# Hymba layer on one core: the second token tile's mixed rows loaded earlier, a clamp joined with the product behind it, one stage's side loads begun later

## The chip, the cores and the metric

The kernel runs on one core of one Trainium2 chip. The metric is the device time of one execution in microseconds (us), the median of several runs. TensorE (PE) multiplies matrices; its weight loads (PEld) overlap with the multiplications. VectorE (DVE), ScalarE (ACT) and GpSimd (POOL) work elementwise, and SyncE (SP) issues the DMAs, each in the order in which they stand in its queue.

## The reference: what is computed

One layer for 1024 tokens of width 1024, float32. A convolution group (256 channels) and an attention group (12 query heads, 4 key heads, head size 64, three gated branches: compressed blocks, selected blocks, sliding window) read the same normalised input. Their outputs are concatenated into the mixed rows, go through one output projection and are added to x; a dense SwiGLU block and a last norm follow.

```python
h = rms_norm(x, attn_norm)
z = h @ w_in
a_conv, q, kc_r, vc_r, ks, vs, kw, vw, g = jnp.split(z, splits, axis=-1)
conv_out = conv_mixer(a_conv, conv_w, conv_b, conv_ln_g, conv_ln_b)
kc = compress(kc_r, cmp_k_pe, cmp_k_w1, cmp_k_w2)
vc = compress(vc_r, cmp_v_pe, cmp_v_w1, cmp_v_w2)
gates = jax.nn.sigmoid(g)
nsa_out = nsa_attention(q, kc, vc, ks, vs, kw, vw, gates)
mix = jnp.concatenate([conv_out, nsa_out], axis=-1)
x = x + mix @ w_out
h = rms_norm(x, ffn_norm)
gate, up = jnp.split(h @ w_gate_up, 2, axis=-1)
return x + (silu(gate) * up) @ w_down
```

## The kernel before

Tokens are cut into eight tiles of 128; tiles 0 to 3 form the first half, 4 to 7 the second. Matrix products are made at higher precision by splitting: an operand is cast to a high part (`w_hi`, `ph`, `ah`; ACT) and the remainder is subtracted (`w_lo`, `pl`, `al`; POOL for weights, DVE for activations), and three matmuls high·high, high·low, low·high replace one. `load_w` (L219 to L237) does this for a weight block: DMA into `w_raw` (L229), cast (L230), subtraction in pieces (L234). Values that cross a stage are written to DRAM and read back: queries `q_d`, keys `ks_d` and `kw_d`, values `vs_d` and `vw_d`, compressed probabilities `pc_d`, and the mixed rows `mix_d[w, channel, token]`, where w is 0 for the high part and 1 for the low one.

The first part of the kernel projects the first half of the tokens (`project_d`, `values`), makes the compressed keys and values (`compress`, `compress_v`) and runs the convolution's end (`conv_tail`, which stores its 256 channels of the mixed rows, L665) with compressed-block scoring (`cmp_stage`, one call for a key group g and a pair of token tiles qt, sixteen in all) beside it. Such side work is given to `drive.side(generator, at)`: `drive.run` steps through the main work, counts its modelled time `drive.t`, and takes a step of a side generator when its due time has come. `cmp_stage` loads queries (L678), makes scores (L686), their minimum over 64 blocks (L693), clamps the six minima to at most CLAMP (L694, tile `cm`), multiplies by the heads' slopes (L696, tile `bm`) and uses the product as bias of the six exponentials on ACT (L700); POOL scales them (L704, L708), PE transposes (L714) and the result goes to `pc_d`.

Then attention over the first half runs, woven with `fill_b`, which yields the projections of the second half and at its end the convolution's input part (`conv_in`). Attention takes one tile and one branch after the other: scores `s` (L851, L855), a reduction with ALiBi on DVE (L859), exponentials on ACT (L866), their sum and reciprocal on DVE (L870, L871), scaling by sum and gate on POOL (L876), transposes `pt` (L882), a split into `ph` and `pl` (L240), the product with the values (L910, L911) beside the compressed branch (L905), and the sum of the branches (`ou`, L914, L915; `oh`, L920, L921), which is stored to `mix_d` (L929). Keys are loaded for each group and branch at L789.

The output projection of the first half (`out_proj`, L1226 `wo`) takes for each token tile twelve matmuls: four blocks of 128 channels, three products. Its rows come from `mix_in` (L1203), which loads tiles 1 to 3 of the high and low part into buffers of the tag `act`, tile 1 first and then tiles 2 and 3 in one piece, and for tile 0 from `first_mix` (L1212), which is called at step 60 of `conv_in` and uses two buffers (`cacc`) of the convolution's pool `py`. The buffers of `act` are the ones in which the normalised input lies until the last matmul of `conv_in`.

Nothing in the code fixes the final order of instructions: a scheduler that simulates a timeline of all engines and queues orders each engine's instructions by its own model. The rows of the order quoted below are its result.

Of the kernel before, what the change touches and what calls it, by code (L numbers as in the profile page):

```python
# [12 lines left out]
F32 = mybir.dt.float32  # L13
# [75 lines left out]
def tile_hymba(ctx: ExitStack, tc, x, attn_norm, w_in, conv_w, conv_b, conv_ln_g, conv_ln_b,  # L89
# [582 lines left out]
    def cmp_stage(g, qt):  # L672
        i0 = qt * 2
        if qt < 2 and g < 3:
            qc = p2.tile([P, REP, 256], F32R, tag="xt", name="qc", bufs=2)
        else:
            qc = t3([P, REP, 256], F32R, "qc", 1)
        sp.dma_start(qc.bitcast(F32), q_d[g * 192:(g + 1) * 192, :, i0 * P:(i0 + 2) * P]  # L678
                     .rearrange("(r d) w t -> (d w) r t", d=HD))
        s = t3([P, 6, 64], F32, "cs", 2)  # L680
        s4 = s.rearrange("p (i r) n -> p i r n", r=REP)
        yield 0.0
        for il in range(2):
            sb = bank("sc", "s")
            for r in range(REP):
                pe.matmul(sb[:, r * P:(r + 1) * P], qc[:, r, il * P:(il + 1) * P], kc[:, g], start=True, stop=True)  # L686
            sb4 = sb[:, :384].rearrange("p (r c n) -> p r c n", r=REP, c=2)
            dve.tensor_tensor(s4[:, il], sb4[:, :, 0, :], cb[:, i0 + il, :].unsqueeze(1).to_broadcast([P, REP, 64]),
                              op=ALU.add)
            dve.tensor_tensor(s4[:, il], s4[:, il], sb4[:, :, 1, :], op=ALU.add)  # L690
        yield 0.7
        m = p1.tile([P, 6], F32, tag="cm", name="cm", bufs=3)
        dve.tensor_reduce(m, s, axis=AX.X, op=ALU.min)  # L693
        dve.tensor_scalar(m, m, CLAMP, None, op0=ALU.min)  # L694
        bm = p1.tile([P, 6], F32, tag="bm", name="bm", bufs=3)
        dve.tensor_tensor(bm.rearrange("p (i r) -> p i r", r=REP), m.rearrange("p (i r) -> p i r", r=REP),  # L696
                          slo[:, g * REP:(g + 1) * REP].unsqueeze(1).to_broadcast([P, 2, REP]), op=ALU.mult)
        l = p1.tile([P, 6], F32, tag="cl", name="cl", bufs=3)
        for u in range(6):
            act.activation(s[:, u, :], s[:, u, :], AF.Exp, scale=-SLOPES[g * REP + u % REP], bias=bm[:, u:u + 1],  # L700
                           accum_out=l[:, u:u + 1])
        dve.tensor_scalar(l, l, 1e-30, None, op0=ALU.max)
        dve.reciprocal(l, l)
        pool.tensor_tensor(s, s, l.unsqueeze(2).to_broadcast([P, 6, 64]), op=ALU.mult)  # L704

        pg = t3([P, 6, 64], F32, "pg", 2)
        gt = gates[:, i0:i0 + 2, g * 9:(g + 1) * 9].rearrange("p i (r b) -> p i r b", b=3)[:, :, :, 0]
        pool.tensor_tensor(pg.rearrange("p (i r) n -> p i r n", r=REP), s4,  # L708
                           gt.unsqueeze(3).to_broadcast([P, 2, REP, 64]), op=ALU.mult)
        yield None  # L710
        pct = t3([P, 3, 2, P], F32R, "pct", 2)
        pt = bank("pt", "t")
        for v in range(3):
            pe.transpose(pt[:, v * P:(v + 1) * P], pg[:, 2 * v:2 * v + 2, :], ident)  # L714
        yield 0.33
        pt3 = pt[:, :384].rearrange("p (v q) -> p v q", q=P)
        for e in range(2):
            src = pt3[e * 64:(e + 1) * 64]
            act.copy(pct[0:64, :, e, :], src)
            dve.tensor_sub(pct[64:128, :, e, :], src, pct[0:64, :, e, :].bitcast(F32))  # L720
        sp.dma_start(pc_d[g, qt], pct.bitcast(F32).rearrange("p v e q -> p (v e q)"))
        done.add(("pc", g, qt))

        if qt < 2:
            return
        im = p1.tile([P, 2, 64], F32, tag="im", name="im", bufs=2)
        pool.tensor_tensor(im, s4[:, :, 0, :], s4[:, :, 1, :], op=ALU.add)
        pool.tensor_tensor(im, im, s4[:, :, 2, :], op=ALU.add)
        ib = p1.tile([P, 2, 16], F32, tag="ib", name="ib", bufs=2)
        im4 = im.rearrange("p i (j n) -> p i j n", n=4)  # L730
        dve.tensor_reduce(ib, im4, axis=AX.X, op=ALU.add)
        dve.tensor_tensor(ib[:, :, 1:16], ib[:, :, 1:16], im4[:, :, 0:15, 3], op=ALU.add)
        dve.tensor_tensor(ib, ib, ft[:, i0:i0 + 2, :], op=ALU.add)
        if qt == 2:
            chosen[g] = p1.tile([P, 4, 16], F32, tag="us", name="us", bufs=2)
        us = chosen[g][:, i0 - 4:i0 - 2, :]
        for il in range(2):
            mx = p1.tile([P, 8], F32, tag="mx", name="mx", bufs=2)
            dve.max(mx, ib[:, il, :])
            dve.match_replace(us[:, il, :], mx, ib[:, il, :], 4.0 * NEG)  # L740
        dve.tensor_tensor(us, us, ib, op=ALU.is_equal)
        if qt == 3:
            yield None
            ut = bank("ut", "t")
            pe.transpose(ut[0:64, :P], chosen[g], ident)
            bt = p1.tile([64, P], F32, tag="im", name="bt", bufs=2)
            yield 0.11
            dve.tensor_scalar(bt, ut[0:64, :P], BIG, None, op0=ALU.mult)
            sp.dma_start(bias_d[g].rearrange("v j q -> (v j) q"), bt)
            done.add(("bias", g))  # L750
# [242 lines left out]
    def stages_in(g):  # L993
        for qt in range(2):
            gaps = iter(STAGE_GAPS)
            for _ in cmp_stage(g, qt):
                yield next(gaps)
# [23 lines left out]
    def mixed_in(a, b):  # L1021
# [31 lines left out]
    turn[1] = "t"  # L1053
    drive.run(in_turn(compress(*xv, first, cmp_v_w2, "z", kv),
                      [project_d(first, dst, r, (0,)) for dst, r in ((ks_d, 0), (kw_d, P))], 24))
    drive.side(stages_in(3))
    drive.run(project_d(first, ks_d, P, (0,)))
    compress_v(*kv)
    p2_stack.close()
# [5 lines left out]
    def fill_b():  # L1065
        f1 = Feed([q_load(0), q_load(1)] + value_loads(C_VS, 0) + [q_load(2)] + value_loads(C_VW, 18)
                  + [q_load(m) for m in (3, 4, 5)] + kv_loads() + conv_loads())
        for m in (0, 1):
            yield from project_d(f1, q_d, m * P, (1,), True)
        yield from values(f1, 0, vs_d, 1)  # L1070
        done.add(("q", 0))
        yield from project_d(f1, q_d, 2 * P, (1,), True)
        done.add(("q", 1))
        yield from values(f1, 18, vw_d, 1)
        done.update({("v", 0), ("v", 1)})
        for m in (3, 4):
            yield from project_d(f1, q_d, m * P, (1,), True)
        done.add(("q", 2))
        yield from project_d(f1, q_d, 5 * P, (1,), True)
        done.add(("q", 3))  # L1080
        for dst in (kw_d, ks_d):
            yield from project_d(f1, dst, 0, (1,))
        done.add(("kv", 0))
        for dst in (kw_d, ks_d):
            yield from project_d(f1, dst, P, (1,))
        done.add(("kv", 1))
        for n, d in enumerate(conv_in(f1, 1)):
            if n == 60:
                first_mix()
            yield d  # L1090
        done.add(("conv", "in"))

# [102 lines left out]
    def mix_in(si, kq, p, tag="act", tokens=True):  # L1195
        assert mixed(si, kq)
        t0, n = SETS[si][0] * P, len(SETS[si]) * P
        mix = [p.tile([P, 4, n], F32R, tag=tag, name="mix", bufs=2) for _ in range(2)]
        src = [mix_d[w, kq * 512:(kq + 1) * 512, t0:t0 + n].rearrange("(k p) t -> p k t", p=P) for w in range(2)]
        for a, b in ((1, 2), (2, 4)) if tokens else ((0, 1), (1, 2), (2, 4)):  # L1200
            for w in range(2):
                if tokens:
                    sp.dma_start(mix[w][:, :, a * P:b * P].bitcast(F32), src[w][:, :, a * P:b * P])  # L1203
                else:
                    sp.dma_start(mix[w][:, a:b, :].bitcast(F32), src[w][:, a:b, :])
        return mix

    def first_mix():
        assert mixed(0, 0)
        for w in range(2):  # L1210
            m = py.tile([P, 4, P], F32R, tag="cacc", name="mix", bufs=2)
            sp.dma_start(m.bitcast(F32), mix_d[w, 0:512, 0:P].rearrange("(k p) t -> p k t", p=P))  # L1212
            ahead.append(m)

    ahead = []

    def out_proj(feed, si, tags, mix, ch, ahead=()):
        ws = [feed.get(), feed.get(1)]
        for t, x1 in enumerate(x1s[si]):
            o = bank("wo", tags[t % len(tags)])  # L1220
            n = 0
            for k in range(4):
                wh, wl = ws[k // 2]
                for a, b in ((0, wh), (0, wl), (1, wh)):
                    rows = ahead[a][:, k, :] if ahead and t == 0 else mix[a][:, k, t * P:(t + 1) * P]
                    pe.matmul(o, rows, b[:, k % 2, :], start=n == 0, stop=n == 11)  # L1226
                    n += 1
                    yield MM
# [481 lines left out]
```

## Time and profile before

| | |
|---|---|
| median of 3 runs | 1431.35 us (1430.51 to 1435.39) |
| profiled execution, its own time | 1432.28 us |
| its span | 1430.6 us |
| mean granted TensorE clock | 0.996 |
| HBM read, written | 160.85 MB, 33.55 MB |

The profile is one execution. Busy time is given for each engine; the rest of the span is idle for it. A line of a view such as `L1226 ... wo<-w_hi,mix` names the source line, the tile written and the tiles read, without buffer numbers. In brackets behind an instruction stands how long its engine was idle before it and which instruction or DMA released it. The PE row of the page, in 40 slices of the span, is full but for the first and the last:

```profile
PE   8999999999999999999999999999999999999997
DMA  7346577676586343343343226723235333233311
```

### The profile page before, as it was taken

The numbers are of one execution on the slowest core, as the hardware profiler recorded it, in microseconds if no ns is written. First come the engines' busy times: TensorE is split into PE (matmuls) and PEld (weight loads), VectorE is DVE, ScalarE is ACT, GpSimd is POOL, SyncE is SP. The second block draws the span as 40 slices with busy tenths as digits, with TensorE's granted clock in tenths as the row PEclk, the third lists the DMA queues.
The fourth block names the chain that finished last, engine by engine and source line by source line (L and its number), as shares of the span: only waits on it lengthen the run. The fifth ranks groups of instructions, "written<-read, shape, count | busy, mean of one in ns | idle before, by whom it ended". The sixth has DMA issues, their size and how long they took to land.

```text
span 1430.6 us, 23380 instructions
## 1 busy us (share of the span) xinstructions
PE 1406.5 (98%) x7941; PEld 1224.0 (86%) x7941; DVE 1030.7 (72%) x2306; ACT 762.7 (53%) x1593; POOL 738.6 (52%) x1043
## 2 busy tenths in 40 slices
PE   8999999999999999999999999999999999999997
PEld 7898888988878888888888888888888999999996
DVE  6488786688976958778687875231658887888874
ACT  6333566678765765656656654214435444444443
POOL 6467775668675667666666666546777000000001
PEclk9999999999999999999999999999999999999999
DMA  7346577676586343343343226723235333233311
GB/s 232 84 132 188 166 210 260 187 232 210 172 277 180 89 118 105 88 123 101 103 127 96 83 68 207 226 80 98 75 117 177 118 116 91 89 105 109 111 60 74
DMA packets 234118, 196.13 MB, mean 137 GB/s; under 512 B 13785, under 2 KB 204093, under 8 KB 233998
## 3 DMA queue, kind: packets, MB, share of 16 engines
q1 hardware_dynamic: 233854, 194.41, 45.3%
q8 instruction: 63, 1.03, 0.3%
q14 instruction: 57, 0.47, 0.1%
q10 hardware_dynamic: 144, 0.23, 0.0%
HBM read 160.85 MB, written 33.55 MB: 136 GB/s over the span
## 4 chain that ended last, share of the span: by engine, by line
PE 89%; DVE 4%; DMA 3%; POOL 2%; ACT 2%; issue 1%; SPq 0%; POOLq 0%; ACTq 0%; DVEq 0%
PE gu L1299 19%; PE dn L1324 17%; PE yy L1455 8%; PE zo L148 6%; PE pt L882 5%; PE zz L1455 4%; PE vo L148 3%; PE zc L148 3%; PE wo L1250 3%; PE wo L1226 3%; PE o L911 3%; PE o L910 3%; PE s L851 3%; PE cv L148 2%; PE aa L1455 2%; PE s L855 2%
## 5 line engine op out<-in xcount | busy, mean ns | idle before, releaser
L234 POOL TENSOR_TENSOR w_lo<-w_raw,w_hi 128x256 fp32r<-128x256 f32 (+1 forms) x508 | 409.9, 839 | 157.4 <-ACT w_hi L230 152.2
L1299 PE MATMUL gu<-h,w_hi 128*128 128x512 f32 x768 | 253.1, 397 | 0.0
L1324 PE MATMUL dn<-w_hi,aw 128*128 128x512 f32 x690 | 240.9, 395 | 0.7 <-DVE af L1306 0.3
L230 ACT CAST w_hi<-w_raw 128x1024 fp32r<-128x1024 f32 (+1 forms) x147 | 152.5, 1050 | 163.4 <-PE gu L1299 61.1
L876 POOL TENSOR_SCALAR pr<-pr,l,gates 128x512 f32<-128x512 f32 (+5 forms) x192 | 144.8, 767 | 97.1 <-DVE l L871 86.9
L866 ACT ACTIVATE pr<-pr,m 128x512 f32<-128x512 f32 (+5 forms) x192 | 136.1, 710 | 101.1 <-DVE m L859 63.3
L240 DVE TENSOR_TENSOR pl<-pt,ph 128x384 fp32r<-128x384 f32 x248 | 133.4, 549 | 52.9 <-ACT ph L240 44.5
L1299 PEld LDWEIGHTS gu<-h,w_hi 128*128 128x128 f32 x768 | 143.4, 188 | 27.7 <-DVE h L240 0.2
L1542 POOL TENSOR_TENSOR rs<-rs,mhalf 128x1 f32<-128x1 f32 x4 | 3.3, 832 | 316.7 <-DVE rs L1541 316.6
L1324 PEld LDWEIGHTS dn<-w_hi,aw 128*128 128x128 f32 x690 | 129.4, 188 | 27.2 <-DVE af L1306 0.9
L1299 PE MATMUL gu<-h,w_lo 128*128 128x512 f32 x384 | 152.5, 397 | 0.0
L1327 DVE TENSOR_TENSOR x<-dn,x 128x512 f32<-128x512 f32 x177 | 118.3, 679 | 47.2 <-PE dn L1324 46.7
L240 ACT CAST ph<-pt 128x384 fp32r<-128x384 f32 x248 | 112.9, 474 | 53.3 <-PE pt L882 29.4
L1324 PE MATMUL dn<-w_lo,aw 128*128 128x512 f32 x345 | 136.2, 395 | 0.0
L882 PE MATMUL pt<-ident,pr 128*128 128x128 f32 x744 | 123.9, 273 | 0.9 <-DVE m L859 0.4
L859 DVE CUSTOM_DVE_ANT_0 pr<-s,base 128x384 f32<-128x384 f32 (+3 forms) x192 | 100.7, 530 | 22.3 <-PE s L853 14.3
L1401 ACT CAST w_s<-sum 128x512 fp32r<-128x512 f32 x80 | 49.3, 621 | 113.6 <-PE yy L1455 94.4
L882 PEld LDWEIGHTS pt<-ident,pr 128*128 128x128 f32 x744 | 93.5, 140 | 17.7 <-issue 1.3
L148 PE MATMUL zo<-h,w_hi 128*128 128x512 f32 x320 | 105.6, 399 | 0.5 <-DVE pct L720 0.3
L851 PE MATMUL s<-kt,q 128*128 128x384 f32 (+3 forms) x288 | 98.7, 346 | 2.1 <-DVE m L859 1.5
L1455 PEld LDWEIGHTS yy<-term,w_s 128*128 128x128 f32 x720 | 93.5, 188 | 5.3
L911 PE MATMUL o<-pl,vt 128*128 128x384 f32 x264 | 94.8, 359 | 0.9 <-DVE pl L240 0.9
(281 smaller groups left out, 3184.6 us busy)
## 6 DMA issues: line engine op xcount, KB each, us to landing
w_raw<-in_w_gate_up_dram SPq DMA_DIRECT2D x48, 512.0 KB, 3.9
w_raw<-in_w_down_dram SPq DMA_DIRECT2D x43, 512.0 KB, 3.6
w_raw<-in_w_in_dram SPq DMA_DIRECT2D x40, 512.0 KB, 4.5
u_raw<-in_w_gate_up_dram SPq DMA_DIRECT2D x20, 512.0 KB, 4.7
g_raw<-in_w_gate_up_dram SPq DMA_DIRECT2D x19, 512.0 KB, 3.8
q_d<-zh SPq DMA_DIRECT2D x12, 512.0 KB, 5.1
qc<-q_d SPq DMA_DIRECT2D x16, 384.0 KB, 4.6
pc_d<-pct SPq DMA_DIRECT2D x16, 384.0 KB, 2.9
```

The source lines that it names most:

```text
L148: lastpe[0] = pe.matmul(*args, **kw)
L230: act.copy(hi[:, :n], raw[:, :n])
L234: eng.tensor_sub(lo[:, q], raw[:, q], hi[:, q].bitcast(F32))
L240: pair = act.copy(hi, src), dve.tensor_sub(lo, src, hi.bitcast(F32))
L851: pe.matmul(sv, q2[0], kk_[:, 0, kk], start=True, stop=False)
L866: act.activation(pr[:, c0:n], pr[:, c0:n], AF.Exp, bias=m, scale=-1.0, accum_out=l3[:, r:r + 1])
L876: pool.tensor_scalar(x_, x_, l3[:, r2:r2 + 1], gates[:, i, c:c + 1], op0=ALU.mult, op1=ALU.mult)
L882: pe.transpose(pt[:, r * P:(r + 1) * P], prs[st][1 + r][:, kk * P:(kk + 1) * P], ident)
L911: pe.matmul(o[:, :384], v, pl, start=False, stop=last)
L1299: pe.matmul(o, w[:, k, :], h2[si][h][k // 4][:, k % 4, :], start=n == 0, stop=n == 3 * KT - 1)
L1324: pe.matmul(o, aws[si][:, a, k, t * P:(t + 1) * P], b[:, 0, h], start=n == 0, stop=n == 5)
L1455: pe.matmul(o, w[:, k, :], h[:, k, :], start=fresh and n == 0, stop=n == 11, skip_group_check=not fresh)
```

## The change

Three edits. `second_mix` is new: at step 76 of `conv_in` it loads tile 1's high and low rows of the first 512 channels, each in two DMAs of 256 channels, into buffers of the convolution's pool (`cn` twice, `m0`, `m1`); `mix_in` then loads only tiles 2 and 3, and `out_proj` takes the rows of tiles 0 and 1 from the list `ahead`. In `cmp_stage`, the clamp and the product become one instruction. The third stage's side loads (`stages_in(3)`) get a due time 4 modelled us later.

```diff
@@ cmp_stage
         dve.tensor_reduce(m, s, axis=AX.X, op=ALU.min)
-        dve.tensor_scalar(m, m, CLAMP, None, op0=ALU.min)
         bm = p1.tile([P, 6], F32, tag="bm", name="bm", bufs=3)
-        dve.tensor_tensor(bm.rearrange("p (i r) -> p i r", r=REP), m.rearrange("p (i r) -> p i r", r=REP),
-                          slo[:, g * REP:(g + 1) * REP].unsqueeze(1).to_broadcast([P, 2, REP]), op=ALU.mult)
+        dve.scalar_tensor_tensor(bm.rearrange("p (i r) -> p i r", r=REP), m.rearrange("p (i r) -> p i r", r=REP),
+                                 CLAMP, slo[:, g * REP:(g + 1) * REP].unsqueeze(1).to_broadcast([P, 2, REP]),
+                                 op0=ALU.min, op1=ALU.mult)
...
-    drive.side(stages_in(3))
+    drive.side(stages_in(3), drive.t + 4.0)
...
             if n == 60:
                 first_mix()
+            if n == 76:
+                second_mix()
...
-        for a, b in ((1, 2), (2, 4)) if tokens else ((0, 1), (1, 2), (2, 4)):
+        for a, b in ((2, 4),) if tokens else ((0, 1), (1, 2), (2, 4)):
...
-            ahead.append(m)
+            ahead.append([m[:, k, :] for k in range(4)])
+
+    def second_mix():
+        for w, tags in enumerate((("cn", "cn"), ("m0", "m1"))):
+            rows = []
+            for c, tag in enumerate(tags):
+                m = py.tile([P, 2, P], F32R, tag=tag, name="mix", bufs=2 if tag == "cn" else 1)
+                sp.dma_start(m.bitcast(F32), mix_d[w, c * 256:(c + 1) * 256, P:2 * P]
+                             .rearrange("(k p) t -> p k t", p=P))
+                rows += [m[:, k, :] for k in range(2)]
+            ahead.append(rows)
...
-                    rows = ahead[a][:, k, :] if ahead and t == 0 else mix[a][:, k, t * P:(t + 1) * P]
+                    rows = ahead[2 * t + a][k] if ahead and t < 2 else mix[a][:, k, t * P:(t + 1) * P]
```

SyncE issues two DMAs more, for the same bytes: two of 128x4x128 less at L1203 (L1205 in the changed kernel), four of 128x2x128 more at L1222. DVE has 16 instructions less. Line numbers of the changed kernel are 2 higher from `fill_b`'s last loop on and 12 higher behind `second_mix`: `wo` of L1226 stands at L1238.

The first place is SyncE's queue around the loads for the output projection. `mix` is the row tile, `x` the residual input, `w_raw` a weight block of the output projection, `oh` attention's output. Before:

```order
L229 DMA w_raw<-in_w_out_dram 128x2x512
L1203 DMA mix<-mix_d 128x4x128
L1203 DMA mix<-mix_d 128x4x256
L929 DMA mix_d<-oh 64x3x128
L1162 DMA x_5680<-in_x_dram 128x512 x2
L229 DMA w_raw<-in_w_out_dram 128x2x512
L1162 DMA x_5680<-in_x_dram 128x512 x2
L818 DMA pct<-pc_d 128x384
L1203 DMA mix<-mix_d 128x4x128
L1203 DMA mix<-mix_d 128x4x256
```

And in the changed kernel:

```order
L229 DMA w_raw<-in_w_out_dram 128x2x512
L929 DMA mix_d<-oh 64x3x128
L1205 DMA mix<-mix_d 128x4x256
L1164 DMA x_5670<-in_x_dram 128x512 x2
L229 DMA w_raw<-in_w_out_dram 128x2x512
L1164 DMA x_5670<-in_x_dram 128x512
L1205 DMA mix<-mix_d 128x4x256
```

The two 128x4x128 loads of tile 1 are gone from here; the second weight block has one load less ahead of it, and the second 128x4x256 load follows it more closely.

The second place is SyncE's queue some 50 rows earlier, between two groups of attention; `kt` are keys. Before:

```order
L789 DMA kt<-kw_d 128x1x512 x2
L486 DMA kw_d<-zh 128x2x512
L929 DMA mix_d<-oh 64x3x128 x2
L818 DMA pct<-pc_d 128x384
L789 DMA kt<-ks_d 128x1x512 x2
```

And in the changed kernel:

```order
L486 DMA kw_d<-zh 128x2x512
L789 DMA kt<-kw_d 128x1x512
L929 DMA mix_d<-oh 64x3x128
L789 DMA kt<-kw_d 128x1x512
L929 DMA mix_d<-oh 64x3x128
L818 DMA pct<-pc_d 128x384
L1222 DMA mix<-mix_d 128x2x128 x2
L789 DMA kt<-ks_d 128x1x512 x2
```

Two of the four new loads stand between the stores of attention's output, which they read, and the load of the selected keys. The other two stand in the queue near the convolution's last stores, one ahead of the first stage's key loads and one behind them.

The third place is GpSimd at the start of attention, where `w_lo` is the remainder of a weight block for the second half's values and `pr` are probabilities that it scales. Before:

```order
L876 TENSOR_SCALAR pr<-pr,l_2618,gates 128x256 x3
L225 CAST w_hi<-l_2618 128x1
L234 TENSOR_TENSOR w_lo<-w_raw,w_hi 128x274 x3
L876 TENSOR_SCALAR pr<-pr,l_2669,gates 128x384 x3
L234 TENSOR_TENSOR w_lo<-w_raw,w_hi 128x274 x5
```

And in the changed kernel:

```order
L876 TENSOR_SCALAR pr<-pr,l_2610,gates 128x256 x3
L225 CAST w_hi<-l_2610 128x1
L876 TENSOR_SCALAR pr<-pr,l_2661,gates 128x384 x3
L234 TENSOR_TENSOR w_lo<-w_raw,w_hi 128x274 x8
```

The three scalings of 128x384 have moved ahead of all eight subtractions. On TensorE the first user of such a remainder stands behind three transposes more:

```order
L148 MATMUL vo<-w_hi,h_129 128x274 x2
L882 MATMUL pt<-ident,pr 128x128 x3
L148 MATMUL vo<-w_lo,h_129 128x274
L148 MATMUL vo<-w_hi,h_133 128x274
L148 MATMUL vo<-w_hi,h_129 128x274
```

was the order there, and now it is:

```order
L148 MATMUL vo<-w_hi,h_129 128x274 x2
L882 MATMUL pt<-ident,pr 128x128 x6
L148 MATMUL vo<-w_lo,h_129 128x274
L148 MATMUL vo<-w_hi,h_133 128x274
L148 MATMUL vo<-w_hi,h_129 128x274
```

Apart from the three moved transposes these rows read alike.

## The prediction

> **What bounds the kernel now.** I read the page first, then busy time and granted clock by stage, then the list of what the matmuls waited for, and then the order of time around the longest wait.
>
> ```profile
> span 1430.6 us, 23380 instructions
> ```
> ```profile
> PE 1406.5 (98%) x7941; PEld 1224.0 (86%) x7941; DVE 1030.7 (72%) x2306; ACT 762.7 (53%) x1593; POOL 738.6 (52%) x1043
> ```
>
> TensorE is busy for 1406.5 of 1430.6 us, so all its idle time together is 24.1 us, or 1.7%. The change neither adds nor removes a matmul. It can gain only from those 24 us and from stretches at a lower clock; it can lose wherever another engine or a queue lets TensorE stop. Columns of the next rows: window, its length, busy time (and instructions) of PE, PEld, DVE, ACT and POOL, granted PE clock, DMA share, GB/s.
>
> ```profile
> 14.00:186.00 172.00, 172.00 (x953) 149.33 (x953) 124.00 (x223) 76.54 (x174) 116.24 (x151) 1.00 0.50 153
> 235.00:245.00 10.00, 8.45 (x48) 7.62 (x48) 8.01 (x39) 9.01 (x28) 5.98 (x15) 0.83 0.57 196
> 398.00:414.00 16.00, 13.29 (x61) 10.57 (x60) 11.63 (x34) 9.07 (x21) 14.58 (x22) 0.89 1.02 341
> 480.00:500.00 20.00, 17.85 (x115) 15.36 (x113) 19.96 (x50) 15.68 (x32) 12.81 (x17) 1.00 0.29 84
> ```
>
> From 14 to 186 us TensorE never stops; 398:414 loses 2.7 us and runs below full clock, at a full DMA system (1.02). What the waits were for (us in total, times, longest):
>
> ```profile
> PE gb L365 <- DMA g<-in_attn_norm_dram: 4.2, 1, 4.2
> PE wo L1226 <- DMA mix<-mix_d: 2.4, 1, 2.4
> PE s L851 <- DVE m L859: 1.5, 1, 1.5
> PE vc L565 <- ACT ah L240: 1.4, 2, 0.9
> PE o L905 <- DVE ou L915: 1.4, 2, 1.2
> ```
>
> The 4.2 us lie at the start, which the change doesn't touch. The second row is the one it aims at.
>
> **Edit 1, tile 1's rows loaded sooner.** First the matmuls there, then the chain, then SyncE's queue (start, us, what):
>
> ```profile
> 406.14 0.40 PE L855 MATMUL s<-kt,q 128*128 128x512 f32 x1
> 408.94 0.73 PE L1226 MATMUL wo<-w_hi,mix 128*128 128x512 f32 x2 [2.40 <-DMA mix<-mix_d]
> 413.28 0.44 PE L905 MATMUL o<-pct,vcs 128*128 128x384 f32 x1
> ```
> ```profile
> 401.10 7.79 DMA mix<-mix_d
> ```
> ```profile
> 401.10 1.96 SPq L1203 DMA_DIRECT2D mix<-mix_d  x2
> ```
>
> Tile 1's rows come in two loads, one for each half of the split; the second is issued only at 401.10 and takes 7.79 us. TensorE stands for 2.40 us. In the changed order those rows are loaded by four smaller DMAs, two beside conv's stores near 210 and 220 us and two near 320 us, some 80 us before use: **−2.4 us**. What L1203 still loads (tiles 2 and 3) moves forward with the (1, 2) piece gone from ahead of it, and its first use stands behind all of tile 1's twelve matmuls.
>
> The stop costs more than itself:
>
> ```profile
> 405.00:410.00 5.00, 2.60 (x14) 1.85 (x13) 2.52 (x8) 3.90 (x8) 5.00 (x9) 1.00 1.09 370
> 410.00:412.00 2.00, 2.00 (x6) 1.52 (x5) 1.02 (x3) 1.04 (x4) 1.09 (x3) 0.52 1.05 406
> 412.00:414.00 2.00, 2.00 (x8) 1.70 (x7) 1.41 (x4) 0.56 (x2) 1.65 (x3) 0.63 1.07 419
> ```
>
> The clock falls just behind it. A mean of 0.52 over 2 us is 1.92 us at half clock, 0.63 is 1.48 us; 3.40 us at half clock lose 1.70 us. It happens once more: 0.83 over the 10 us of 235:245 is again 3.4 us, after 1.55 us of idle in that window. The 2.15 us of idle in 480:500 (longest 1.5) drew none, so about 1.5 us of idle close together is where it starts. With the stop gone: **−1.7 us** (0 if another stop takes its place).
>
> The Trainium skill ("TensorE: Matmul & The Clock Gate", Part 1, What's actually happening) has the clock halve after at least one idle window of about 3.4 us, in windows that run free of the kernel. The length agrees with the 3.40 us above; the idle that it asks for doesn't, since 2.40 us sufficed here. By its rule the halved stretch would not hang on this stop, and the edit would give 2.4 us alone; I go by the rows.
>
> What is late next there:
>
> ```profile
> 406.02 1.05 ACT L230 CAST w_hi<-w_raw 128x1024 fp32r<-128x1024 f32 x1 [2.70 <-DMA w_raw<-in_w_out_dram]
> 409.27 0.55 DVE L915 TENSOR_TENSOR ou<-o,ou 64x384 f32<-64x384 f32 x1
> ```
>
> TensorE would reach L905 at 413.28 − 2.4 − 1.7 = 409.2 us, while the accumulator that it needs is emptied at 409.27 + 0.55 = 409.8 (L905 already waits on L915 elsewhere). That is 0.6 us, less what ScalarE gains from its weights arriving with one load fewer ahead of them. **+0.3 us**, between 0 and 1.0 (the 1.05 us cast at the head of ScalarE's queue).
>
> The new loads also stand in SyncE's queue and wait there: for their buffers, and for the stores of the rows that they read. The first two lie ahead of attention's first keys:
>
> ```profile
> L851 PE MATMUL s<-kt,q x288: 218/336/667, 230.5 to 838.5; 128*128 128x384 f32 x84, 128*128 128x512 f32 x36, 128*128 128x128 f32 x12, 128*128 128x256 f32 x12
> ```
> ```profile
> L789 SPq DMA_DIRECT2D kt<-kw_d x16: 550/570/1558, 210.9 to 721.3; - x16
> ```
> ```profile
> DMA to landing us min/median/max: 3.9/4.6/6.3
> ```
>
> These are the instructions that use the key tile; behind a colon stand durations in ns and the first and last start, below them the landing times of its loads. The keys go at 210.9 and are first used at 230.5; landing in 6.3 us, they could go 13 us later, and the loads and one store now ahead of them take a few. That is hidden. The last two new loads stand behind the stores of attention's output (L929) and ahead of the next stage's selected keys (L789):
>
> ```profile
> 315.24 2.58 SPq L929 DMA_DIRECT2D mix_d<-oh  x2
> ```
> ```profile
> 319.16 1.20 SPq L789 DMA_DIRECT2D kt<-ks_d  x2
> ```
> ```profile
> mix_d<-oh SPq DMA_DIRECT2D x62, 96.0 KB, 3.2
> ```
> ```profile
> kt<-ks_d SPq DMA_DIRECT2D x12, 256.0 KB, 5.1
> ```
> ```profile
> 326.11 0.30 PE L851 MATMUL s<-kt,q 128*128 128x128 f32 x1
> ```
>
> Now the second key load goes at about 319.8 and lands at 324.9, 1.2 us before use. After: the second store goes by 317.0 (GpSimd makes its tile ahead of one prescaling), lands 3.2 us on at 320.2, two loads of some 0.55 us issue, and the keys go at 321.3 and 321.9: landed at 327.0, 0.9 us late. I take **+0.6 us**; the ends are 0 (the store lands as its neighbours do and TensorE comes later) and 2.5 (it takes 1.7 us longer, as the median of the key loads does against that of the stores).
>
> **Edit 2, the clamp.** Columns: count, shortest/median/longest in ns, first and last start.
>
> ```profile
> L694 DVE TENSOR_SCALAR cm<-cm x16: 152/170/3070, 146.1 to 393.8; 128x6 f32<-128x6 f32 x16
> ```
> ```profile
> L696 DVE TENSOR_TENSOR bm<-cm,slo x16: 147/172/996, 148.2 to 395.1; 128x6 f32<-128x6 f32 x16
> ```
> ```profile
> 289.28 3.07 DVE L694 TENSOR_SCALAR cm<-cm 128x6 f32<-128x6 f32 x1
> ```
> ```profile
> 289.50 2.83 POOL L234 TENSOR_TENSOR w_lo<-w_raw,w_hi 128x256 fp32r<-128x256 f32 x4
> ```
> ```profile
> 292.87 0.44 PE L851 MATMUL s<-kt,q 128*128 128x384 f32 x1 [0.53 <-DVE pl L240]
> ```
>
> Sixteen DVE instructions go; at the median that is 16 × 0.17 = 2.7 us of an engine with 28% to spare. Only where one is stretched does it reach TensorE: at 289.28 the clamp ends with four GpSimd subtractions beside it, and TensorE waits 0.53 us behind it. The joined instruction does both steps in one and meets GpSimd once where two did. **−0.3 us**, between −0.6 (that wait and a little of another) and +0.5 (the joined one is caught there in its turn: the product's longest is 1.0 us).
>
> The Trainium skill ("SBUF — State Buffer", Who interferes with whom) says that a VectorE instruction with both inputs in SBUF, as well as one in a two-port mode, can be shut out for the whole of a GpSimd instruction. That speaks against the join: its product still has both inputs in SBUF, and the term would be 0. The trace has 3.07 us for the clamp and at most 1.0 us for the product, so I stay between.
>
> **Edit 3 and the reshuffle.** The third stage's loads begin later, and with the other edits the planner puts out another order from about 200 us on. At 244 us GpSimd now runs one head's prescaling (L876) before three weight remainders (L234), whose first user on TensorE hardly moves:
>
> ```profile
> 243.96 0.17 DVE L871 RECIPROCAL l<-l 128x3 f32<-128x3 f32 x1
> ```
> ```profile
> 244.12 2.25 POOL L234 TENSOR_TENSOR w_lo<-w_raw,w_hi 128x274 fp32r<-128x274 f32 x3 [0.67 <-ACT w_hi L230]
> 246.35 1.94 POOL L876 TENSOR_SCALAR pr<-pr,l,gates 128x384 f32<-128x384 f32 x3
> ```
> ```profile
> 245.13 0.37 PE L148 MATMUL vo<-w_lo,h 128*128 128x274 f32 x1
> ```
>
> The prescaling can start at 243.96 + 0.17 = 244.13 and ends 1.94 later, at 246.07; the first remainder is there 0.75 later, at 246.8. TensorE, with three more transposes ahead (0.11 each), asks for it at 245.5: 1.3 us of wait. **+1.2 us**, between 0 (TensorE comes that much later) and 1.4. At the two waits for compressed values (1.4 us together) TensorE's order now has other work ahead of them, but ScalarE's has more exponentials ahead of the casts that they await: 0, between −1.4 and +1.0. At attention's start, 1.55 us of idle and 3.4 us at half clock may repeat or not: 0, between −1.7 and +0.4.
>
> **Sum:** −2.4 − 1.7 + 0.3 + 0.6 − 0.3 + 1.2 = −2.3 us. The profiled execution took 1432.28 us, its span of 1430.6 and 1.7 around it; that gives 1430.0. The median of the runs shown is 0.9 lower, so **1429.1 us** (−0.16%).
>
> **Rivals.** (1) Further up the order fewer stops draw the half clock: attention's 1.55 us is close to the 1.5 that drew none. Then −1.7 there, no wait for keys or for the remainders (−1.8), and part of the 1.4 for compressed values: about 1425.0. For it: the margin is small. Against: nothing in the new order shortens ScalarE's work there. (2) The stop is only replaced. GpSimd is busy 5.00 of 5 us in 405:410, so the prescaling and with it the transposes set the pace; L905 and its neighbours give back 2 us and more: 1431.3. Against: VectorE and ScalarE had 2.5 and 1.1 us idle there. (3) Slower: SyncE's queue is held by the new loads at 320 us. If the stores need 1.7 us more than their 3.2, TensorE stands 2.5 us for the keys, which is over the 1.5 that draws 1.7 us of half clock: 4.2 instead of 0.6, a sum of +1.3, or 1432.7; it turns slower once that place costs over 2.9. With another half clock behind the 1.3 us at 245 it is 1434.4, and with attention's stops worse as well it passes 1435.6. (4) The change doesn't do what it says: the last new loads wait so long that tile 1's rows are no earlier; with 80 us between, hardly: 1431.4.
>
> **How the numbers follow.** Chances: the forecast (1427.3 to 1431) 0.42, rival 1 0.25, rival 2 0.13, rival 3 0.17, rival 4 0.03. The range, 1424.4 to 1433.6, leaves out the far ends of rivals 1 and 3, a tenth each. About 0.3%, 4.3 us, is what a measurement of this kernel can tell from no change. Faster by more (below 1427.05) is most of rival 1 and a sixth of the forecast: 0.30; slower by more is over half of rival 3: 0.11; within it 0.59.
>
> **What would show it.** Right: no wait for mix at L1226, granted clock 1.00 behind it, a wait of at most 1 us at L905; a wait of about 1.3 us for w_lo near 246 us and one under 1 us at the first scores of the stage near 326. The clamp is right if no VectorE instruction of that line lasts as long as GpSimd's block beside it. The sum is wrong if TensorE's idle time in 398:414 stays above 1.5 us, if half-clock stretches are other than one, or if idle appears after 440 us, for which I have no term.

## The result and the profile after

The changed kernel is slower: 1443.27 us (median of 5 runs, 1439.88 to 1449.88) against 1432.12 (5 runs), a ratio of 1.0073 with a 95% interval of 1.0046 to 1.0100. Forecast were 1429.1 us and a range that ended at 1433.6. Run again on another occasion, the same kernel stands at 1.0060 (1.0035 to 1.0084). Its page and the list of what its matmuls waited for (us in total, times, longest):

```profile
span 1443.4 us, 23353 instructions
...
PE 1407.4 (98%) x7941; PEld 1224.1 (85%) x7941; DVE 1039.5 (72%) x2290; ACT 765.7 (53%) x1593; POOL 735.2 (51%) x1043
```
```profile
PE s L851 <- DVE m L859: 6.6, 2, 6.2
PE pt L882 <- DVE m L859: 5.4, 4, 2.5
PE gb L365 <- DMA g<-in_attn_norm_dram: 4.2, 1, 4.2
PE o L910 <- ACT ph L240: 1.9, 2, 1.4
PE dn L1336 <- DVE af L1318: 1.5, 2, 1.2
PE wo L1238 <- DVE y L590: 1.3, 1, 1.3
```

The wait for mix has gone from the list, and VectorE stands at its head. Busy time by stage, first of before for the one window that was not shown, then after:

```profile
500.00:880.00 380.00, 379.23 (x2022) 326.26 (x2021) 289.96 (x715) 233.56 (x423) 249.48 (x362) 1.00 0.36 101
```
```profile
235.00:245.00 10.00, 7.34 (x47) 6.07 (x45) 7.40 (x36) 8.45 (x27) 5.65 (x14) 1.00 0.54 201
398.00:414.00 16.00, 14.03 (x74) 11.49 (x73) 15.12 (x35) 9.41 (x23) 12.85 (x20) 1.00 1.00 341
480.00:500.00 20.00, 13.71 (x80) 12.41 (x78) 18.02 (x28) 11.98 (x24) 7.71 (x13) 0.83 0.23 69
500.00:880.00 380.00, 371.94 (x1975) 318.80 (x1975) 290.52 (x704) 230.29 (x415) 239.43 (x352) 1.00 0.33 97
```

The place that the change aims at gained: 398:414 has 0.7 us more TensorE work in it, at full clock. The loss lies where no edit works: none of the changed lines runs in these stretches. TensorE idles 8.1 us in 500:880 (0.8 before) and 6.3 in 480:500 (2.15), with 6.8 us at half clock there, which lose 3.4 (a mean of 0.83 over 20 us). VectorE is as busy in 500:880 as before (290.5 and 290.0 us), so more work there is not the reason; its results come too late. (Over the whole span it is 8.8 us busier than before, with 16 instructions fewer; the kernel without the clamp, below, loses as much with VectorE busy for 1031.7 us, 1.0 more than before, so that sum is not the reason either.) The largest wait, on VectorE, GpSimd and TensorE:

```profile
481.40 6.84 DVE L254 SCALAR_TENSOR_TENSOR rows<-x,rs,rows 128x1024 f32<-128x1024 f32 x1
```
```profile
481.13 2.81 POOL L234 TENSOR_TENSOR w_lo<-w_raw,w_hi 128x256 fp32r<-128x256 f32 x4
483.89 0.54 POOL L895 TENSOR_SCALAR_AFFINE_SELECT pl<-pl 128x384 fp32r<-128x384 f32 x1
484.38 2.78 POOL L234 TENSOR_TENSOR w_lo<-w_raw,w_hi 128x256 fp32r<-128x256 f32 x4
```
```profile
488.96 0.69 PE L851 MATMUL s<-kt,q 128*128 128x384 f32 x1 [6.15 <-DVE m L859]
```

A normalisation product with both inputs in SBUF, 1.28 us at its shortest, lasts 6.84: it starts 0.3 us into a back-to-back run of nine GpSimd instructions, and ends 1.1 us after the run's end (484.38 + 2.78 = 487.16), which is nearly its own length. The reduction (L859) is queued behind it, and TensorE's next scores wait for that.

### The profile page after: what moved, and what is told of

Same layout as the page of the kernel before. It is cut to its first block, busy times and chain, and to the rows that moved or that the text cites. A ratio compares the mean times of both kernels' runs of the same rounds, so it can differ in the third digit from the quotient of the medians.

```text
span 1443.4 us, 23353 instructions
## 1 busy us (share of the span) xinstructions
PE 1407.4 (98%) x7941; PEld 1224.1 (85%) x7941; DVE 1039.5 (72%) x2290; ACT 765.7 (53%) x1593; POOL 735.2 (51%) x1043
## 4 chain that ended last, share of the span: by engine, by line
PE 77%; DVE 9%; POOL 4%; DMA 4%; ACT 3%; issue 2%; SPq 0%; POOLq 0%; DVEq 0%; ACTq 0%
PE dn L1336 16%; PE gu L1311 16%; PE yy L1467 8%; PE pt L882 4%; PE zz L1467 4%; PE zo L148 3%; PE vo L148 3%; PE wo L1238 3%; PE o L910 3%; PE o L911 3%; PE s L851 3%; PE cv L148 2%; PE wo L1262 2%; DVE cacc L613 2%; POOL w_lo L234 2%
## 5 line engine op out<-in xcount | busy, mean ns | idle before, releaser
L859 DVE CUSTOM_DVE_ANT_0 pr<-s,base 128x384 f32<-128x384 f32 (+3 forms) x192 | 101.5, 533 | 33.3 <-PE s L855 20.0
L910 PE MATMUL o<-ph,vt 128*128 128x384 f32 x264 | 96.4, 365 | 1.9 <-ACT ph L240 1.9
```

Source lines behind the costliest of these rows:

```text
L910: pe.matmul(o[:, :384], v, ph, start=False, stop=False)
```

## The experiments

**Three edits apart.** The obvious rival to an accident of timing is that one edit costs. Each alone, and the whole once more. The edits are the parts of the diff above.

> Edit 1 alone (tile 1's rows loaded sooner; clamp and stage as before). Its own effect, by the prediction: no wait for mix at the projection, no half clock behind it, 2.4 + 1.7 = 4.1 us less in 398 to 414. Theory A: beyond 440 us the order differs from before's in any case, so the total is a new draw between -4 and +8 us. Rival C (edit 1's loads in SyncE's queue cost the 11 us): about 1443 us, with waits that follow late loads.

> Edit 2 alone (clamp joined with the product). Own effect: 16 VectorE instructions less, 0 to -0.6 us. The wait for mix at the projection (2.4 us and the half clock) stays. Theory A: a new draw of the order as a whole, -3 to +10 us, and where it is slow, the waits stand beside long VectorE instructions with SBUF inputs only. Rival D (the joined instruction itself is caught): stretched instructions at the joined line, up to 16 x 3 us of VectorE time.

> Edit 3 alone (third stage's side loads 4 modelled us later). It moves 7 rows of TensorE's order, 8 of VectorE's, none of GpSimd's. Theory A: nearly the same order, so 1431 to 1434 us, the same waits as before within 1 us. Rival: if the moved loads themselves cost, a wait for keys or queries at attention's start (230 to 245 us) and up to +3 us.

> The changed kernel once more, nothing edited. Theory A (VectorE instructions with both inputs in SBUF are shut out while GpSimd works back to back, and where that falls depends on moments of the run): its time is again 1440 to 1450 us, and its profile shows 6.2 us of wait at 482 us again only if the same instruction is caught; other places may be caught instead, with 15 to 20 us of stretched VectorE time in all. Rival B (the order itself starves TensorE at 482, 544 and 657 us): all three waits recur within 0.5 us each.

| kernel | median us | ratio to before | 95% interval | rows of TensorE's order that differ from before |
|---|---|---|---|---|
| edit 1 alone | 1429.71 | 0.9995 | 0.9984 to 1.0006 | 28 |
| edit 2 alone | 1445.26 | 1.0108 | 1.0088 to 1.0129 | 2338 |
| edit 3 alone | 1430.96 | 1.0003 | 0.9991 to 1.0014 | 5 |
| all three, again | 1439.16 | 1.0060 | 1.0035 to 1.0084 | 2341 |

(The last column compares TensorE's 7941 rows in the traces place by place, by operation, tile names and shapes; the expectations' counts differ from it by up to 16 rows. Before's median beside these is 1430.34.) Of the three edits taken alone, only the join loses, and only the join moves the order much; what the edits do together comes below. Edit 1's order, which was expected to differ behind 440 us, has its last moved row at 423. Rival C falls: the loads alone cost nothing. The repeat decided between A and B in halves: in its profile the 6.2 us at 482 are gone (1.6 us idle in 480:500), as A had it, but 500:880 idles 8.5 us (8.1 in the first profile) at the same instructions, as B had it. Edit 1's own stage does what was predicted, in its one profile:

```profile
398.00:414.00 16.00, 15.60 (x86) 13.17 (x85) 13.30 (x38) 11.28 (x29) 15.34 (x23) 1.00 0.99 354
```

**The instruction or the order.** Two kernels separate them. One keeps the clamp and puts the joined instruction in the product's place; every engine's order is that of before. The other takes the clamp out and keeps the old product; every engine's order is that of the join.

```diff
 # twice: before's order, the joined instruction
         dve.tensor_scalar(m, m, CLAMP, None, op0=ALU.min)
-        dve.tensor_tensor(bm..., m..., slo..., op=ALU.mult)
+        dve.scalar_tensor_tensor(bm..., m..., CLAMP, slo..., op0=ALU.min, op1=ALU.mult)
 # no clamp: the join's order, the old product
-        dve.tensor_scalar(m, m, CLAMP, None, op0=ALU.min)
         dve.tensor_tensor(bm..., m..., slo..., op=ALU.mult)
```

> The kernel before with the clamp kept and the product replaced by the joined instruction (it clamps a second time, which changes no value). Every engine's order is that of before, row for row; only 16 VectorE instructions are another kind. If the joined instruction itself costs (rival D), this is 1440 to 1446 us. If the order that follows from one instruction less costs (theory A), this is before's time within 0.3%, 1427 to 1435 us.

> The kernel before with the clamp left out and the product as it was (what is left out: the limit on the block scores' minima). Every engine's order is that of the join alone, row for row, with the old product in place of the joined instruction. Theory A: the join's time, 1443 to 1448 us, with VectorE stretched again near 543 and 654 us. Rival D: 1430 us.

The first measured 1431.9 us, a ratio of 0.9995 (0.9981 to 1.0009); the second 1445.45, 1.0102 (1.0076 to 1.0127). The instruction costs nothing; the order costs 1%. The old product without the clamp loses nearly what the join does (1.0102 against 1.0108). Its 500:880 idles 7.5 us and the join's 8.1, first the kernel without the clamp, then the join:

```profile
500.00:880.00 380.00, 372.51 (x1983) 320.04 (x1982) 291.88 (x707) 229.91 (x416) 239.87 (x353) 1.00 0.34 97
500.00:880.00 380.00, 371.87 (x1985) 319.93 (x1984) 292.72 (x706) 231.03 (x418) 237.02 (x350) 1.00 0.33 96
```

The joined instruction in before's order idles 0.7 there:

```profile
500.00:880.00 380.00, 379.34 (x2024) 326.88 (x2023) 290.24 (x717) 233.76 (x424) 249.02 (x362) 1.00 0.36 101
```

So with sixteen instructions of some 0.17 us less, in 146 to 395 us, the planner puts out another order, up to about row 4485 of TensorE's 7941, which before has at 828 us. The changed kernel, its repeat, the join alone and the kernel without the clamp have one order from some 560 us on.

**What is slow in that order.** In the join's kernel the two largest waits of 500:880 follow one pattern. VectorE first, then GpSimd, then TensorE:

```profile
543.16 3.90 DVE L613 SCALAR_TENSOR_TENSOR cacc<-y,c,cacc 128x512 f32<-128x512 f32 x1 [1.03 <-POOL c L610]
546.98 0.55 DVE L859 CUSTOM_DVE_ANT_0 pr<-s,base 128x384 f32<-128x384 f32 x1
```
```profile
543.20 0.53 POOL L895 TENSOR_SCALAR_AFFINE_SELECT pl<-pl 128x384 fp32r<-128x384 f32 x1
543.68 2.82 POOL L234 TENSOR_TENSOR w_lo<-w_raw,w_hi 128x256 fp32r<-128x256 f32 x4
```
```profile
547.59 0.55 PE L882 MATMUL pt<-ident,pr 128*128 128x128 f32 x3 [2.30 <-DVE m L859]
```

A product of the convolution (0.75 us at the median) waits for a tiny copy on GpSimd, starts as that ends, and meets GpSimd's next run at its first instruction: 3.90 us, until 0.6 us after the run. The same happens at 654 us, with 1.86 us of wait. These two products last 3.9 and 4.4 us in all four profiles of that order, the kernel without the clamp included. A long product alone is no loss: before has one of 3.30 us at 753 and idles 0.8 us in 500:880. VectorE's wait for GpSimd was measured by itself, in a kernel with nothing else:

```python
pool.tensor_copy(c, acc[:, 0:3])
dve.scalar_tensor_tensor(two[:, :lead], pt[:, :lead], c[:, 0:1], y[:, :lead], op0=ALU.mult, op1=ALU.add)
work(c)      # 128x512 product, 128x3 clamp, or 128x512 product with PSUM for one input
for k in range(n):
    pool.tensor_sub(lo[:, q], raw[:, q], hi[:, q].bitcast(F32))
```

> No layer: a measurement of the disputed wait by itself (everything of the reference is left out). GpSimd makes a 128x3 copy that releases one VectorE instruction, and then 0, 4 or 8 subtractions of 128x256; VectorE's instruction comes at once or behind a lead instruction of 64 to 512 columns that reads PSUM. Theory A: with both inputs in SBUF (128x512 product, 128x3 clamp) some of the instructions last until the whole run of 4 or 8 subtractions is over (about 2.9 or 5.8 us and more), at others only until the subtraction under way ends (up to 0.7 us more); with PSUM for one input none is stretched. Rival E (VectorE never waits for more than one GpSimd instruction): no instruction over 1.6 us.

It took 290.95 us in its one execution. Line 115 is the product, 118 the clamp (whose one input lies in SBUF), 121 the product that reads PSUM, each 27 times, nine of them without subtractions behind the copy (shortest/median/longest in ns):

```profile
L115 DVE SCALAR_TENSOR_TENSOR acc<-y,c,acc x27: 740/797/1346, 6.2 to 98.1; 128x512 f32<-128x512 f32 x27
```
```profile
L118 DVE TENSOR_SCALAR l<-c x27: 157/274/5232, 103.5 to 185.3; 128x3 f32<-128x3 f32 x27
```
```profile
L121 DVE SCALAR_TENSOR_TENSOR acc<-pt,c,acc x27: 740/743/751, 190.2 to 274.3; 128x512 f32<-128x512 f32 x27
```
```profile
144.73 5.23 DVE L118 TENSOR_SCALAR l<-c 128x3 f32<-128x3 f32 x1
```

With one input in PSUM none is stretched. With SBUF alone most of those beside subtractions wait for the one under way, up to 0.6 us, and three of the nine clamps beside runs of eight last 4.8 to 5.2 us, until the run is over. Rival E falls. No 128x512 product was caught for a whole run here, and none of the clamps beside runs of four; what decides between one GpSimd instruction and the whole run stays open.

Then the two copies were moved to ScalarE in the join's kernel:

```diff
-                    pool.tensor_copy(c2, pace[-1])
-                    pool.tensor_copy(c2, cols[...])
+                    act.copy(c2, pace[-1])
+                    act.copy(c2, cols[...])
```

> The join alone, and the two tiny copies that release each pair of convolution products (128x3) moved from GpSimd to ScalarE, so that VectorE isn't released at the edge of a GpSimd run. Theory A: the stretches of 3.15 and 3.63 us at the convolution's products go, and with them the waits of 2.3 and 1.6 us and some half clock: 4 to 7 us less than the join alone, 1438 to 1441 us, unless the order that follows puts others in their place. If the waits near 543 and 654 us stay as long without the stretches, theory A is wrong there.

The longest such product is now 1.58 us (4.38 in the join's kernel), and the waits of 2.3 and 1.9 us are gone. The total is not better: 1447.06 us, 1.0104 (1.0085 to 1.0124). The order moved once more, and 500:880 idles 7.6 us at other places, the longest 1.8 us for a split (`pl`) on VectorE at 609. The chain above shows the stretches as the cause of those two waits; taking both away was worth nothing in total. As TensorE's order is another from 532 us on, what the stretches alone cost stays open.

**The order put back.** If the order is the cause, a number that has nothing to do with the join should mend it. Two were found that bring the order of the later stages back to that of before, row for row, with all three edits in place; edits 2 and 3 without 1 do so too, and 1 and 3 hardly leave it. (Edits 1 and 2 without 3 were not run.)

```diff
 # six
-    drive.side(stages_in(3), drive.t + 4.0)
+    drive.side(stages_in(3), drive.t + 6.0)
 # tail
-    drive.side(conv_tail(0), drive.t + 10.0)
+    drive.side(conv_tail(0), drive.t + 11.0)
```

> All three edits, with one number changed: the third stage's side loads 6 modelled us later instead of 4. In the order, TensorE's rows behind attention's first part (from about 440 us on) are then those of before again, row for row; 1055 rows ahead of that differ, 2325 in the changed kernel. Theory A' (the loss comes from the order of 500 to 880 us that the join brings about, not from any work that the edits add): TensorE's idle time in 500 to 880 falls from about 8 us to 1, no half clock there, and the total is 1426 to 1432 us. Rival F (the loss follows from the edits wherever the order goes): 1439 to 1446 us.

> All three edits as they are, and another number changed: the convolution's tail is due 11 modelled us after its place instead of 10, which has nothing to do with the clamp, the rows or the third stage. TensorE's order from about 440 us on is again that of before. Theory A': 1426 to 1432 us. Rival F: 1439 to 1446 us.

> Edits 2 and 3 without edit 1. TensorE's order from about 440 us on is that of before, though the join is in it and alone it isn't. Theory A': before's time within 0.3%, with the wait for mix at the projection still there. Rival D (the join costs): 1440 to 1446 us.

> Edits 1 and 3 without the join: 33 rows of TensorE's order differ from before. Theory A': no loss behind 440 us, no wait for mix, 1426 to 1431 us. If the 4.1 us that the profile shows at the wait for mix are real in every execution, it is faster than before by 0.2 to 0.3%; edit 1 alone was within 0.16%, which spoke against that.

| kernel | median us | ratio to before | 95% interval | idle in 500:880, one profile | rows of TensorE's order that differ from before |
|---|---|---|---|---|---|
| three edits, six | 1436.37 | 1.0022 | 1.0006 to 1.0039 | 0.5 | 1062, the last at 546 us |
| three edits, tail | 1436.65 | 1.0030 | 1.0013 to 1.0048 | 4.4 | 1158, the last at 546 us |
| edits 2 and 3 | 1432.64 | 0.9997 | 0.9981 to 1.0014 | 1.7 | 570, the last at 423 us |
| edits 1 and 3 | 1431.45 | 0.9984 | 0.9972 to 0.9997 | 0.8 | 33, the last at 423 us |

(Before's median beside these is 1431.99; the last column has before's time of the last row that differs.) The expectations put the return too early for the first two: their rows are before's from 546 us on, not from 440. One number of the planner takes off 0.3 to 0.5% of the 0.6 to 0.7% by the medians of the ratios, in two kernels that have one order with each other from 226 us on, so that the one stands beside the other as a second trial; rival F, which had 1439 us and more, falls with it. Both still miss the expected 1426 to 1432: ahead of 546 us their order is not before's, and in the profile of "six" 245:280 idles 2.5 us (0.2 before). The join with edit 3 has no loss that can be measured, so rival D falls a second time. It also shows that the loss isn't the join's alone. With edits 2 and 3 in place it is edit 1, which by itself moves 28 rows, that moves 1787 rows of TensorE's order, from 403 us of the changed kernel on, and brings the loss. What the slow kernels share is the later order, and no single edit. The wait for mix in edits 2 and 3, expected to stay, was 0.4 us: in their order the load is issued at 398.95, not 401.10, without edit 1. In 500:880 "six" idles 0.5 us and "tail" 4.4, with the same order; "six" first:

```profile
500.00:880.00 380.00, 379.53 (x2039) 327.90 (x2038) 295.09 (x722) 236.15 (x429) 245.74 (x358) 1.00 0.35 99
500.00:880.00 380.00, 375.63 (x2005) 323.86 (x2004) 295.14 (x712) 232.67 (x422) 240.28 (x355) 1.00 0.34 98
```

The "tail" kernel shows why, at 599 us, where its rows on TensorE, VectorE and GpSimd are before's; VectorE first, then GpSimd and TensorE:

```profile
598.86 4.23 DVE L613 SCALAR_TENSOR_TENSOR cacc<-y,c,cacc 128x512 f32<-128x512 f32 x1 [1.48 <-POOL c L610]
603.01 0.68 DVE L1318 TENSOR_TENSOR af<-gu,af 128x512 f32<-128x512 f32 x1
```
```profile
599.73 2.81 POOL L234 TENSOR_TENSOR w_lo<-w_raw,w_hi 128x256 fp32r<-128x256 f32 x4
```
```profile
603.74 0.50 PE L1336 MATMUL dn<-w_hi,aw 128*128 128x512 f32 x1 [2.97 <-DVE af L1318]
```

3.0 of its 4.4 us of idle time come from one product caught behind GpSimd. In "six" the same product, in the same order, waits as long for its copy and is not caught:

```profile
600.46 0.98 DVE L613 SCALAR_TENSOR_TENSOR cacc<-y,c,cacc 128x512 f32<-128x512 f32 x1 [1.47 <-POOL c L610]
```

Edits 1 and 3 are the version that beats both kernels, by 0.16% on before (0.03 to 0.28):

```profile
398.00:414.00 16.00, 15.96 (x88) 13.46 (x87) 13.64 (x40) 12.39 (x32) 15.66 (x24) 1.00 1.03 368
500.00:880.00 380.00, 379.22 (x2023) 326.70 (x2022) 286.24 (x705) 233.94 (x423) 249.22 (x364) 1.00 0.37 105
```

## Why the prediction was wrong

**The step that failed** is "Edit 3 and the reshuffle": "the third stage's loads begin later, and with the other edits the planner puts out another order from about 200 us on". It took the reshuffle for a common effect, priced it at three places ahead of 330 us, and left everything behind 440 us at nothing ("for which I have no term"). Alone, only the join, priced at −0.3 us, makes a large reshuffle; the three together have the join's later order, and edits 2 and 3 without 1 do not. Most of the reshuffle's price falls in 480:880: in the changed kernel's profile 4.1 us more idle time and 3.4 lost at half clock in 480:500, and 7.3 more idle in 500:880. Another 3.4 us at half clock, from 675 us on, lose 1.7. These 16.5 us are more than the 12.8 by which the span grew; the place of the mix gives back 2.5 (0.7 of idle time and 1.8 of half clock), and 235:245 gives back 0.6 (1.7 of half clock, less 1.1 of idle time more). Why that order leaves TensorE waiting is shown for three waits, at 482, 547 and 659 us, where VectorE is held beside GpSimd, and not for the rest. The margin there could be read from before: TensorE idled 0.8 us in 380 with VectorE 76% and GpSimd 66% busy, an order that fits closely. The two other orders seen there, the join's and that with the copies on ScalarE, idle 7.5 us and more, and before's own idles 4.4 in "tail".

**Edit 1, −2.4 and −1.7 us.** The mechanism was right, and in one execution the size. In the profile of edits 1 and 3 the wait is gone, the clock behind it is 1.00, and the span is 1426.0, 4.6 us under before's; that execution is the fastest of its twelve. Over the runs the gain is 2.3 us (0.4 to 4.0, from the ratio), and of edit 1 alone 0.7 (−0.9 to 2.3): at the medians smaller than the 4.1. One possible reason, not shown for these runs, is that the half clock doesn't follow every such stop: it is absent behind 2.0 us of wait in the kernel without the clamp.

**What is late next there, +0.3.** L905 waits for L915 as foreseen, 0.65 us. Ahead of it the changed kernel has a new 1.3 us: a 128x3 clamp of attention's sums (L870) lasted 3.62 us beside GpSimd and held the convolution's last product, for which the first matmul of the projection waits. In the repeat, and with edit 1 alone, it isn't there.

**New loads in SyncE's queue, +0.6.** Near in size by luck. The two loads wait 2 us for the stores, but those go earlier (313.72 instead of 315.24 with two), and the keys are issued at 318.84, 0.3 us sooner than before. TensorE's wait at the first scores is 0.7 us, and not for the new loads: edits 2 and 3 without them have the same 0.7 there, and edits 1 and 3 with them have none, though the keys go at 320.40, 1.2 us later than before. Rival 3 was not what made the kernel slower. (Its bound of 1.7 us was misread too: the two medians that it names, 5.1 and 3.2, are 1.9 apart.)

**The remainders at 245 us, +1.2.** The mechanism was right, and the size a third: 0.4 us, since TensorE came 2 us later than before, after 2.7 us of idle in 235:245 (1.55 before), where the term was 0. The waits for compressed values, also put at 0, came to 0.8 us, from 1.4.

**Edit 2, −0.3.** As an instruction it is worth nothing that can be measured: 0.9995 in before's order. As an edit of the program it costs 1% alone, and nothing beside edit 3 (0.9997). The joined instruction lasted 2.72 us near 175 in six profiles, behind a run of GpSimd (the longest in this one is 0.74). The Trainium skill ("SBUF — State Buffer", Who interferes with whom) says that a VectorE instruction with two SBUF inputs contends with a GpSimd instruction that reads SBUF; the 2.72 us agree.

**The clock.** 6.8 us at half clock followed the wait of 6.15 us; none followed the 2.66 us of idle time in 235:245, which lay in pieces, nor the wait of 2.54 us in one piece at 547. The stop of 1.5 us near 487 is followed by half clock with edit 3 alone (a mean of 0.91 in 480:500) and not in before (1.00). The 3.4 us at half clock from 675 on follow 1.6 us of idle time in 672:676 (2.35 of 4 us busy), in pieces. All fit the estimate of about 1.5 us close together as a need, and the stops that draw none show that it isn't enough.

## What to carry to other kernels

Where a planner sets the order, price an edit by what it does to the order, and count that for each edit alone and for the edits together. Alone they moved 28, 2338 and 5 rows; edit 3 took most of edit 2's move back, and edit 1 on top of both brought it again, so the counts do not add and the order to price is the final one. A kernel that keeps TensorE busy for 98% of its span can stand on an order that fits closely; here sixteen small instructions taken out in front of it cost more than they saved, and a number that shifts the plan back is worth trying before the edit is given up. A stretched instruction that is found in the slower kernel's profile may be the cause of its wait and still not be what the time hangs on: take it away and measure the total.

## What the runs showed of the hardware

A VectorE instruction with SBUF inputs alone can be held for a whole run of GpSimd instructions, and not only for one: 6.84 us instead of 1.28 beside nine of them, 5.23 instead of 0.16 for three columns in the small kernel. With one input in PSUM all 18 beside such runs kept 0.74 to 0.75 us. The same order gives both outcomes: 6.2 us of wait at 482 and none of that size in the repeat of the same kernel; 4.23 and 0.98 us at 599 in two kernels that have one order from 226 us on. That may be a part of why the changed kernel's five runs are spread over 10 us.
